# Batched attention-times-value on one core: v loaded in rows of 16 KiB and spread by zero-padded matrices

## Chip, core and metric

The kernel runs on one core of a Trainium2 chip. The metric is the device time in microseconds (us) of one execution; the time of before is the median of three runs.

## The reference

```python
def setup_inputs():
    batch, n_heads, seq, head_dim = 8, 12, 1024, 64
    return {
        "attn_weights": np.random.randn(batch, n_heads, seq, seq).astype(np.float32),
        "v": np.random.randn(batch, n_heads, seq, head_dim).astype(np.float32),
    }

def reference(attn_weights, v):
    return np.einsum('bhqs,bhsd->bhqd', attn_weights, v).astype(np.float32)
```

For each of the 96 heads the kernel multiplies a 1024 x 1024 matrix by a 1024 x 64 matrix, all float32 in memory: 402.7 MB of attention weights and 25.2 MB of v are read, and 25.2 MB of output are written.

## The kernel before

**Units.** The heads are taken in 24 batches (`q`) of four. In a batch each head owns 32 partitions, and each partition holds 32 consecutive query rows of its head. A batch is worked in two units, even and odd (`n` = 0 to 47, `i = n % 2`), of 16 query rows per partition each. `load_attn(n)` (L324) brings a unit's rows as one transfer on Pool's queue that casts from float32 to bfloat16 on its way, 8.4 MB read and 4.2 MB written, into one of two buffers `abf`. Units 46 and 47 are loaded in two halves.

**A unit on TensorE (PE).** `pe_unit` (L186) waits for the unit's load, then transposes it in 16 groups of four matmuls (`transpose_g`, L129, matmuls at L134). VectorE (DVE) and ScalarE (ACT) copy the transposed groups out of PSUM in turns (`copy_g`, L255). PE then transposes the outputs of the unit before back (`transpose_back`, L161), ACT copies these to `osb` (L238), and PE multiplies the transposed weights by v (`multiply`, L176): for each head and each half of the queries eight matmuls accumulate, the two halves going to two halves of the PSUM partitions.

**v.** The matmuls need v as `vbf`, with the position in the sequence, taken modulo eight pieces, on 128 partitions. It is loaded otherwise, in long rows of memory: a partition of `vr` holds 32 consecutive rows of one head, 8 KiB of float32, and a load has two batches side by side (`[P, 2, VB, SB * D]`). `spread_v` (L144) moves it to 128 partitions: for each head, on that head's 32 partitions, four matmuls with 32 x 128 selection matrices (`spread`, of zeros and ones) accumulate in one PSUM bank (L149); the four heads use the four groups of 32 rows of the PE array. It runs once in each even unit, between the unit's transposes and the transposes back. After each head's last matmul `s_sp` goes up by one; DVE copies heads 0 and 2 to `vbf`, ACT heads 1 and 3 (`spread_copy`, L231), and `transpose_back` of that unit waits for all four.

**Pool's queue, in program order.** After the first two attn loads and the selects that build `ident` and `spread`, Pool goes through the units. At an even unit of an odd batch it first waits for that batch's fourth `s_sp`, then issues the next v load (`load_v`, L332, 11 of them); then, for every unit, it waits for DVE's part of the transposes and issues the attn load of two units later. Outputs of eight batches are stored in bursts at batches 8 and 16; the stores of the last batches are issued at the end, on Pool's queue and on SyncE's (SP's).

**The first v.** Its two batches come as float32 on SP's queue, into room of `osb` that is not yet used (`v32`). The first 1 MiB is issued ahead of everything; the memsets of DVE, Pool's selects and ACT's start wait for it. DVE casts it to `vr`. The second 1 MiB is issued by SP after that, and Pool casts it (L382) after it has issued the attn load of unit 2.

Of the kernel before, what the change touches and what calls it, by code (L numbers as in the profile page):

```python
# [10 lines left out]
def kernel(  # L11
# [18 lines left out]
    nc = tc.nc  # L30
    fp32 = mybir.dt.float32
    bf16 = mybir.dt.bfloat16
    PE, DVE, ACT = (getattr(mybir.EngineType, x) for x in ("PE", "DVE", "Activation"))

    B, H, Q, S = attn_weights.shape
    D = v.shape[-1]
    NH = B * H
    P = 128
    VH = 4
    VP = P // VH  # L40
# [2 lines left out]
    HP = P // 2  # L43
    KW = S // (2 * P)
    SB = S // P
    VB = S // VP // SB
    NV = NH // VH
    NU = 2 * NV

# [6 lines left out]
    V_SLOT = 4  # L56
# [5 lines left out]
    def slot(q):  # L62
        return q % NO
# [5 lines left out]
    def out_n(q, fours):  # L69
# [1 line left out]
            "(n four) (p r) d -> (four p) n (r d)", four=VH, p=VP  # L71
        )

    v_2 = v.rearrange("b h q d -> (b h) q d").rearrange(
        "(hq two four) (p r) d -> hq (four p) two (r d)", two=2, four=VH, p=VP
    )

    def on_dve(g):
# [9 lines left out]
    sem = tc.alloc_semaphore  # L88
    sb = lambda name, shape, dt: nc.alloc_sbuf_tensor(name, shape, dt).ap()
    ident = sb("ident", [P, P], fp32)  # L90
    spread = sb("spread", [P, VB, P], bf16)
    abf = [sb(f"abf{i}", [P, G, S], bf16) for i in range(2)]
    at = sb("at", [P, G, KW, P, 2], bf16)
    vr = sb("vr", [P, 2, VB, SB * D], bf16)
    vbf = sb("vbf", [P, SB, VH, D], bf16)
    ot = sb("ot", [P, GH, P], fp32)
    osb = sb("osb", [P, NO, 2 * G, D], fp32)

    v32 = osb[:, ds(V_SLOT, 2)].rearrange("p n r d -> p n (r d)")
    bank = [nc.alloc_psum_tensor(f"bank{i}", [P, 512], fp32).ap() for i in range(8)]  # L100
    pt = [b.rearrange("p (k j) -> p k j", k=KW) for b in bank[:4]]
    po = bank[4:6]
# [2 lines left out]

    s_abf = [sem(f"s_abf{i}") for i in range(2)]
    s_second = {n: sem(f"s_second{n}") for n in range(HALVED, NU)}
    s_v0, s_v = sem("s_v0"), sem("s_v")
    s_osb = sem("s_osb")
    s_held, s_end = sem("s_held"), sem("s_end")  # L110

# [8 lines left out]
    s_const, s_vr = sem("s_const"), sem("s_vr")  # L120

    s_half, s_free = sem("s_half"), sem("s_free")

    nc.sync.dma_start(out=v32[:, 0], in_=v_2[0][:, 0])

    with tc.tile_critical(sync_engine=mybir.EngineType.Pool, no_gpsimd_drain=True):  # L126
        pe = nc.tensor
# [16 lines left out]
        def spread_v(two, banks):  # L144

            for h, ps in enumerate(banks):
                rows = ds(h * VP, VP)
                for b in range(VB):
                    last = pe.matmul(  # L149
                        out=ps,  # L150
                        lhsT=spread[rows, b],
                        rhs=vr[rows, two, b],
                        start=(b == 0),
                        stop=(b == VB - 1),
                    )
                last.then_inc(s_sp)
# [29 lines left out]
        def pe_unit(i, n, both, loaded, it):  # L186

            pe.wait_ge(*loaded)
            for g in range(G):
                if g == GH:  # L190
                    pe.wait_ge(s_half, n)
                transpose_g(abf[i], g, n)
            pe.wait_ge(s_ot, both)
            if i == 0:
                pe.wait_ge(s_vr, it)
                odd = pe.snap((it - 1) % 2)
                with pe.If(odd > 0):
                    spread_v(1, po + px)
                with pe.Else():
                    spread_v(0, po + px)  # L200
                pe.wait_ge(s_vbf, it * 4)
            transpose_back()
            pe.wait_ge(s_last, both)
            for hp in range(2):
                for h in range(2):
                    for half in range(2):
                        outs = po[hp][ds(half * D, D), ds(h * GH * VP, GH * VP)]
                        last = multiply(outs, 2 * hp + h, half)
                last.then_inc(s_m)

        pe.wait_ge(s_const, 3 + VH)
        with nc.Fori(1, NV + 1, 1, engines=(PE,)) as it:
            loaded = pe.snap(it * 16)
            second = pe.snap(it * 2)
# [95 lines left out]
            nc.vector.memset(ot[:, :, ds(h * HP, HP)], 0.0).then_inc(s_ot)  # L310
        for half in range(2):
            last = nc.vector.tensor_copy(
                out=vr[:, 0, ds(half * (VB // 2), VB // 2)].rearrange("p b x -> p (b x)"),
                in_=v32[:, 0, ds(half * (SB * D * VB // 2), SB * D * VB // 2)],
            )
        last.then_inc(s_vr)
        engine(True)
        engine(False)
        nc.scalar.wait_ge(s_held, 16 * (BY_SYNC - HELD_FROM) // 2)
# [2 lines left out]
        pool = nc.gpsimd  # L322

        def load_attn(n):  # L324
            pieces = [(0, G)] if n < HALVED else [(0, GH), (GH, GH)]
            for g0, gn in pieces:
                pool.dma_start(  # L327
                    out=abf[n % 2][:, ds(g0, gn)].rearrange("p g s -> p (g s)"),
                    in_=attn_q[n // 2][:, ds((n % 2 * G + g0) * S, gn * S)],
                ).then_inc(s_abf[n % 2] if g0 == 0 else s_second[n], 16)  # L330

        def load_v(iv):  # L332
            pool.dma_start(  # L333
                out=vr.rearrange("p two b x -> p two (b x)"), in_=v_2[iv]
            ).then_inc(s_v, 16)

        def store(q, fours, eng, done):
            eng.wait_ge(s_out, 2 * (q + fours) + 1)
            at_slot = osb[:, ds(slot(q), fours)].rearrange("p n r d -> p n (r d)")
            eng.dma_start(  # L340
                out=out_n(q, fours), in_=at_slot,
                **({"single_packet": True} if eng is pool and fours == 2 else {}),
            ).then_inc(done, 16)

        def store_2(q):
# [7 lines left out]
            out=ident,  # L353
            in_=ident,
            compare_op=mybir.AluOpType.not_equal,
            fill=1.0,
            base=0,
            pattern=[[-1, P]],
            channel_multiplier=1,
        ).then_inc(s_const)  # L360

        for h in range(VH):
            pool.wait_ge(s_const, h + 3)
            pool.affine_select(  # L364
                out=spread[ds(h * VP, VP)],
                in_=spread[ds(h * VP, VP)],
                compare_op=mybir.AluOpType.not_equal,
                fill=1.0,
                base=0,
                pattern=[[1, VB], [-1, P]],  # L370
                channel_multiplier=VB,
            ).then_inc(s_const)
        for n in range(NU - 2):
            q, i = n // 2, n % 2
            if i == 0 and q % 2 == 1 and q + 1 < NV:
                pool.wait_ge(s_sp, 4 * (q + 1))
                load_v((q + 1) // 2)
            pool.wait_ge(s_t[True], (n + 1) * PER_DVE)
            load_attn(n + 2)
            if n == 0:  # L380
                pool.wait_ge(s_v0, 16)
                pool.tensor_copy(  # L382
                    out=vr[:, 1].rearrange("p b x -> p (b x)"), in_=v32[:, 1]
                ).then_inc(s_vr)
            if i == 0 and q % TOGETHER == 0 and 0 < q <= HELD_FROM:
                for q0, fours in BURSTS[q]:
                    store(q0, fours, pool, s_osb)
# [5 lines left out]

        nc.sync.dma_start(out=v32[:, 1], in_=v_2[0][:, 1]).then_inc(s_v0, 16)
        nc.sync.sem_inc(s_free, NO // 2)
        nc.sync.sem_inc(s_half, HALVED)
        for k in range(1, NV // 2):
# [6 lines left out]
        for n in range(HALVED, NU):  # L406
# [8 lines left out]
            out=out_q[NV - 1], in_=osb[:, slot(NV - 1)].rearrange("p r d -> p (r d)")  # L415
# [35 lines left out]
```

## Time and profile before

| | |
|---|---|
| time, median of 3 runs | 1052.8 us (1052.76 to 1053.04) |
| profiled execution: its own time | 1052.94 us |
| profiled execution: span | 1051.2 us |
| PE busy, mean granted clock | 731.1 us (70%), 0.866 |
| DVE, ACT, Pool busy | 388.2, 410.3, 44.6 us |
| HBM read, written | 427.82 MB, 25.17 MB |
| packets of Pool's queue (q0) | 12832, 99.2% of the 16 DMA engines' span |
| packets of SP's queue (q1) | 848, 1.5% |
| attn load, issue to landing (median) | 30.9 us |
| v load, issue to landing (median) | 12.5 us |

A line of a group gives source line, engine, operation, tiles and shapes, the number of instructions, then busy time in us, the mean of one in ns, and the engine's idle time just before them with what ended it. A line of the timeline gives start and duration in us, and in brackets the idle time before. PEld is PE's loading of weights, which overlaps its matmuls. The queues' lines give packets, MB written and the time of their packets as a share of 16 DMA engines over the span. The sizes of a DMA are those written, after the cast.

### The profile page before, as it was taken

What the parts mean: (1) busy time and instruction counts of PE and PEld (TensorE: products, weight loads), DVE (VectorE), ACT (ScalarE), POOL (GpSimd) and SP (SyncE); (2) the same over time, 40 slices, a digit from 0 to 9 for tenths busy, and PEclk for the clock granted to TensorE, in tenths of its full rate; (3) what the DMA queues carried; (4) which work ended last, traced back from release to release, by engine and by line L of the source; (5) the groups of instructions that cost most, each with busy time, mean ns of one, the idle gap of its engine ahead of it and who ended that gap; (6) DMA issues with size and microseconds to landing.
All of it is one profiled execution on the core that took longest, in us unless ns stands there. A gap on an engine that the chain in (4) does not pass through costs nothing.

```text
span 1051.2 us, 16374 instructions
## 1 busy us (share of the span) xinstructions
PE 731.1 (70%) x6920; PEld 686.2 (65%) x6920; DVE 388.2 (37%) x583; ACT 410.3 (39%) x493; POOL 44.6 (4%) x76
## 2 busy tenths in 40 slices
PE   0877688679579576457957858758716875875985
PEld 0767687578478575457857758658716865875874
DVE  1443344335335333233523434335303433532543
ACT  0444345335335333233533434335304433533543
POOL 2000000000000000000000000001000000000000
PEclk9989889889889898688989889889868988988898
DMA  9999999999999999999999999999999999999998
GB/s 233 227 220 217 218 218 208 216 219 219 219 217 218 216 207 379 219 219 217 217 216 208 219 219 219 207 229 217 359 225 219 219 206 229 218 206 218 218 218 343
DMA packets 13685, 240.19 MB, mean 228 GB/s; under 512 B 1136, under 2 KB 1136, under 8 KB 3952
## 3 DMA queue, kind: packets, MB, share of 16 engines
q0 software_dynamic: 12832, 233.84, 99.2%
q1 hardware_dynamic: 848, 6.29, 1.5%
q8 instruction: 2, 0.03, 0.0%
q14 instruction: 3, 0.02, 0.0%
HBM read 427.82 MB, written 25.17 MB: 431 GB/s over the span
## 4 chain that ended last, share of the span: by engine, by line
DMA 78%; PE 20%; issue 1%; POOL 0%; DVE 0%; ACT 0%; POOLq 0%; SPq 0%
DMA abf<-in_attn_weights_dram 78%; PE bank L134 20%; PE bank L176 0%; PE bank L161 0%; POOL abf L327 0%; DVE osb L238 0%; ACT ot L267 0%; SPq L408 0%; POOLq L435 0%; POOLq L126 0%
## 5 line engine op out<-in xcount | busy, mean ns | idle before, releaser
L134 PE MATMUL bank<-ident,abf 128*128 128x128 f32 x3072 | 446.8, 315 | 277.6 <-DMA abf<-in_attn_weights_dram 273.6
L134 PEld LDWEIGHTS bank<-ident,abf 128*128 128x128 f32 x3072 | 437.3, 214 | 290.4 <-DMA abf<-in_attn_weights_dram 285.8
L255 DVE COPY at<-bank 128x1024 bf16<-128x1024 bf16 x480 | 320.4, 689 | 486.8 <-PE bank L134 484.2
L255 ACT COPY at<-bank 128x1024 bf16<-128x1024 bf16 x288 | 288.8, 1012 | 411.9 <-PE bank L134 411.9
L176 PE MATMUL bank<-at,vbf 128*64 128x256 bf16 x3072 | 215.0, 278 | 0.0
L176 PEld LDWEIGHTS bank<-at,vbf 128*64 128x64 bf16 x3072 | 196.7, 108 | 13.4 <-DVE at L255 4.0
L267 ACT COPY ot<-bank 128x512 f32<-128x512 f32 x48 | 28.1, 586 | 174.0 <-PE bank L176 174.0
L267 DVE COPY ot<-bank 128x512 f32<-128x512 f32 x48 | 33.2, 692 | 151.4 <-PE bank L176 151.4
L161 PE MATMUL bank<-ident,ot 128*128 128x128 f32 x392 | 52.2, 276 | 32.5 <-DVE vbf L231 31.9
L161 PEld LDWEIGHTS bank<-ident,ot 128*128 128x128 f32 x392 | 43.4, 141 | 44.6 <-DVE vbf L231 43.7
L238 ACT COPY osb<-bank 128x512 f32 (+1 forms) x97 | 52.1, 589 | 27.3 <-PE bank L161 26.2
L327 POOL DMA_DIRECT2D abf<-in_attn_weights_dram x50 | 27.1, 542 | 716.9 <-PE bank L134 716.0
L231 DVE CAST vbf<-bank 128x512 bf16<-128x512 f32 x48 | 30.9, 686 | 6.5 <-PE bank L149 6.5
L231 ACT CAST vbf<-bank 128x512 bf16<-128x512 f32 x48 | 25.8, 589 | 11.8 <-PE bank L149 11.8
L149 PE MATMUL bank<-vr,spread 32*128 32x512 bf16 x384 | 26.1, 377 | 0.0
L255 ACT ACT_TABLE_LOAD x12 | 15.4, 1283 | 6.1 <-DMA osb<-in_v_dram 5.9
L333 POOL DMA_DIRECT2D vr<-in_v_dram x11 | 7.7, 703 | 228.7 <-PE bank L149 228.7
L149 PEld LDWEIGHTS bank<-vr,spread 32*128 32x128 bf16 x384 | 11.0, 92 | 6.2
L340 POOL DMA_DIRECT2D out_dram<-osb x5 | 3.9, 785 | 6.9 <-ACT osb L238 6.6
L364 POOL TENSOR_SCALAR_AFFINE_SELECT spread<-spread 32x512 bf16<-32x512 bf16 x4 | 3.6, 900 | 0.6
L306 DVE MEMSET ident<- 128x128 f32 x1 | 0.2, 165 | 5.9 <-DMA osb<-in_v_dram 5.9
L382 POOL CAST vr<-osb 128x2048 bf16<-128x2048 f32 x1 | 1.9, 1883 | 0.0
(9 smaller groups left out, 4.3 us busy)
## 6 DMA issues: line engine op xcount, KB each, us to landing
abf<-in_attn_weights_dram POOLq DMA_DIRECT2D x46, 4096.0 KB, 30.9
vr<-in_v_dram POOLq DMA_DIRECT2D x11, 1024.0 KB, 12.5
out_dram<-osb POOLq DMA_DIRECT2D x1, 8192.0 KB, 44.5
abf<-in_attn_weights_dram POOLq DMA_DIRECT2D x4, 2048.0 KB, 24.0
out_dram<-osb POOLq DMA_DIRECT2D x3, 2048.0 KB, 35.8
out_dram<-osb POOLq DMA_DIRECT2D x1, 6144.0 KB, 44.9
osb<-in_v_dram SPq DMA_DIRECT2D x2, 1024.0 KB, 14.4
out_dram<-osb SPq DMA_DIRECT2D x1, 2048.0 KB, 13.9
```

The lines of the kernel that those rows point to most:

```text
L134: last = pe.matmul(out=pt[g % 4][:, k], lhsT=words[:, k], rhs=ident, is_transpose=True, start=(k == 0), stop=(k == KW - 1),)
L149: last = pe.matmul(out=ps, lhsT=spread[rows, b], rhs=vr[rows, two, b], start=(b == 0), stop=(b == VB - 1),)
L161: last = pe.matmul(out=ps[:, ds(j * P, P)], lhsT=ot[:, j0 + j], rhs=ident, is_transpose=True, start=(j == 0), stop=(j == jn - 1),)
L176: last = pe.matmul(out=outs, lhsT=vbf[:, 2 * kw + par, h], rhs=at[:, ds(half * GH, GH), kw, ds(h * VP, VP), par], start=(n == 0), stop=(n ...
L231: copy(out=vbf[:, :, h], in_=ps.rearrange("p (k d) -> p k d", k=SB)).then_inc(s_vbf)
L238: return copy(out=rows.rearrange("p (half j) d -> p j half d", half=2)[:, ds(j0, jn)], in_=ps[:, ds(0, jn * P)].rearrange("p (j half d) -> ...
L255: ins = copy(out=at[:, g].rearrange("c k j two -> c (k j two)"), in_=bank[g % 4].bitcast(bf16),)
L267: copy(out=ot.rearrange("c j (h p) -> c h j p", h=VH)[:, ds(2 * e, 2)], in_=po[e].rearrange("c (h j p) -> c h j p", h=2, j=GH),).then_inc( ...
L327: pool.dma_start(out=abf[n % 2][:, ds(g0, gn)].rearrange("p g s -> p (g s)"), in_=attn_q[n // 2][:, ds((n % 2 * G + g0) * S, gn * S)],).th ...
L333: pool.dma_start(out=vr.rearrange("p two b x -> p two (b x)"), in_=v_2[iv]).then_inc(s_v, 16)
L340: eng.dma_start(out=out_n(q, fours), in_=at_slot, **({"single_packet": True} if eng is pool and fours == 2 else {}),).then_inc(done, 16)
L364: pool.affine_select(out=spread[ds(h * VP, VP)], in_=spread[ds(h * VP, VP)], compare_op=mybir.AluOpType.not_equal, fill=1.0, base=0, patte ...
```

## The change

A load of v now has eight heads on 128 partitions: 16 partitions a head, each with 64 consecutive rows, 16 KiB of float32 (`v_8`). `vr` loses its dimension of two batches and has eight pieces (`VB` = 8) instead of four. A head's 16 partitions are half of a group of 32, so `spread_v` still takes 32 rows and a selection matrix in which the rows of the other head in that group are zero: `spread` is now `[P, 8, 135]`, one zero-padded band for each of the eight heads, and the matrix for piece `b` is a window of 128 columns in it that starts at `VB - 1 - b`. Each head takes eight matmuls instead of four. In one batch, heads 0 and 1 lie in one group of 32 rows and heads 2 and 3 in another.

The first v comes as one transfer of 2 MiB, ahead of everything, and DVE casts all of it in two instructions of 2048 elements per partition; SP's second transfer and Pool's cast go. One select on Pool over 128 partitions builds `spread` in place of four over 32.

```diff
-    VB = S // VP // SB
+    V8 = 2 * VH
+    VB = S // (P // V8) // SB
+    VR = 32
...
-    v_2 = v.rearrange("b h q d -> (b h) q d").rearrange(
-        "(hq two four) (p r) d -> hq (four p) two (r d)", two=2, four=VH, p=VP
+    v_8 = v.rearrange("b h q d -> (b h) q d").rearrange(
+        "(ho eight) (p r) d -> ho (eight p) (r d)", eight=V8, p=P // V8
     )
...
-    spread = sb("spread", [P, VB, P], bf16)
+    spread = sb("spread", [P, V8, P + VB - 1], bf16)
...
-    vr = sb("vr", [P, 2, VB, SB * D], bf16)
+    vr = sb("vr", [P, VB, SB * D], bf16)
...
-    v32 = osb[:, ds(V_SLOT, 2)].rearrange("p n r d -> p n (r d)")
+    v32 = osb[:, ds(V_SLOT, 2)].rearrange("p n r d -> p (n r d)")
...
-    nc.sync.dma_start(out=v32[:, 0], in_=v_2[0][:, 0])
+    nc.sync.dma_start(out=v32, in_=v_8[0])
...
             for h, ps in enumerate(banks):
-                rows = ds(h * VP, VP)
+                j = two * VH + h
+                rows = ds(j * (P // V8) // VR * VR, VR)
                 for b in range(VB):
                     last = pe.matmul(
                         out=ps,
-                        lhsT=spread[rows, b],
-                        rhs=vr[rows, two, b],
+                        lhsT=spread[rows, j, ds(VB - 1 - b, P)],
+                        rhs=vr[rows, b],
...
-        pe.wait_ge(s_const, 3 + VH)
+        pe.wait_ge(s_const, 4)
...
             last = nc.vector.tensor_copy(
-                out=vr[:, 0, ds(half * (VB // 2), VB // 2)].rearrange("p b x -> p (b x)"),
-                in_=v32[:, 0, ds(half * (SB * D * VB // 2), SB * D * VB // 2)],
+                out=vr[:, ds(half * (VB // 2), VB // 2)].rearrange("p b x -> p (b x)"),
+                in_=v32[:, ds(half * (SB * D * VB // 2), SB * D * VB // 2)],
             )
-        last.then_inc(s_vr)
+        last.then_inc(s_vr, 2)
...
-                out=vr.rearrange("p two b x -> p two (b x)"), in_=v_2[iv]
+                out=vr.rearrange("p b x -> p (b x)"), in_=v_8[iv]
...
-        for h in range(VH):
-            pool.wait_ge(s_const, h + 3)
-            pool.affine_select(
-                out=spread[ds(h * VP, VP)],
-                in_=spread[ds(h * VP, VP)],
+        pool.wait_ge(s_const, 3)
+        pool.affine_select(
+            out=spread,
+            in_=spread,
...
-            if n == 0:
-                pool.wait_ge(s_v0, 16)
-                pool.tensor_copy(
-                    out=vr[:, 1].rearrange("p b x -> p (b x)"), in_=v32[:, 1]
-                ).then_inc(s_vr)
...
-        nc.sync.dma_start(out=v32[:, 1], in_=v_2[0][:, 1]).then_inc(s_v0, 16)
```

More of the change, by code (lines that the diff above doesn't have):

```diff
@@ L107 @@
     s_second = {n: sem(f"s_second{n}") for n in range(HALVED, NU)}
-    s_v0, s_v = sem("s_v0"), sem("s_v")
+    s_v = sem("s_v")
     s_osb = sem("s_osb")
@@ L360 @@
         ).then_inc(s_const)
-        for h in range(VH):
-            pool.wait_ge(s_const, h + 3)
-            pool.affine_select(
-                out=spread[ds(h * VP, VP)],
-                in_=spread[ds(h * VP, VP)],
[L367 to L372, printed above, removed]
+        pool.wait_ge(s_const, 3)
+        pool.affine_select(
+            out=spread,
+            in_=spread,
+            compare_op=mybir.AluOpType.not_equal,
+            fill=1.0,
+            base=VB - 1,
+            pattern=[[-P, V8], [-1, P + VB - 1]],
+            channel_multiplier=VB,
+        ).then_inc(s_const)
         for n in range(NU - 2):
```

## The prediction

> **What bounds the kernel now.** I read the page first (slices and DMA queues), then the chain, then two stretches of the timeline, then the list of who waited for whom.
>
> ```profile
> PE 731.1 (70%) x6920; PEld 686.2 (65%) x6920; DVE 388.2 (37%) x583; ACT 410.3 (39%) x493; POOL 44.6 (4%) x76
> DMA  9999999999999999999999999999999999999998
> q0 software_dynamic: 12832, 233.84, 99.2%
> q1 hardware_dynamic: 848, 6.29, 1.5%
> DMA 78%; PE 20%; issue 1%; POOL 0%; DVE 0%; ACT 0%; POOLq 0%; SPq 0%
> ```
>
> The 16 DMA engines are full in every slice. Bytes confirm it: 427.8 MB read by loads and 25.2 MB stored are 453 MB, 431 GB/s over the span. PE is busy for 70% and waits 273.6 us for attn loads, so PE, DVE and ACT have room, and the time is that of the DMA queue, provided that the queue never runs empty. That proviso is where this change can hurt, so I looked at one v load (unit 26 of 48):
>
> ```profile
> 579.71 10.32 PE L134 MATMUL bank<-ident,abf 128*128 128x128 f32 x64 [4.63 <-DMA abf<-in_attn_weights_dram]
> ...
> 589.96 1.07 PE L149 MATMUL bank<-vr,spread 32*128 32x512 bf16 x16
> ...
> 591.47 0.70 POOL L333 DMA_DIRECT2D vr<-in_v_dram  x1 [20.85 <-PE bank L149]
> 592.17 0.56 POOL L327 DMA_DIRECT2D abf<-in_attn_weights_dram  x1
> 592.38 0.86 PEld L161 LDWEIGHTS bank<-ident,ot 128*128 128x128 f32 x8 [1.84 <-DVE vbf L231]
> ...
> 599.00 1.24 PE L134 MATMUL bank<-ident,abf 128*128 128x128 f32 x8 [1.12 <-DMA abf<-in_attn_weights_dram]
> ```
>
> An attn load lands at 579.7, PE transposes it, spreads v (L149), and only then does Pool issue the next v and, behind it, the next attn load. The load before them lands at 599.0: DMA still had some 7 us of work when v was issued. The packet records say it closer: the first v packet runs 5.8 to 6.2 us after the issue in nine of the eleven loads. In the other two (407 and 756) a store is queued ahead and the figure is 25.8.
>
> ```profile
> L149 PE MATMUL bank<-vr,spread 32*128 32x512 bf16 x384 | 26.1, 377 | 0.0
> L149 PEld LDWEIGHTS bank<-vr,spread 32*128 32x128 bf16 x384 | 11.0, 92 | 6.2
> ...
> vr<-in_v_dram POOLq DMA_DIRECT2D x11, 1024.0 KB, 12.5
> ```
>
> These page lines hold what the change touches: 384 spread matmuls, 16 for each of 24 batches of four heads, together busy for only 26.1 us although one lasts 377 ns, so they overlap; and eleven v loads, 12.5 us from issue to landing, half of it waiting in the queue.
>
> **v's packets.** Eleven loads go from 256 packets (8 KiB read, 4 KiB written) to 128 of twice the size: per engine from 16 to 8. A unit's attn load without v takes 19.3 us (599.00 - 579.71) for 8 packets of 64 KiB per engine, 2.412 us each; with v the step is 24.22 (unit 28 starts at 623.22), so v costs 4.90 us, 0.306 per packet. Bytes are then 37.6 ns per KiB and a packet's own cost is 5 ns. Eight packets fewer save 0.04 us a load, 0.5 us in eleven. The packets' recorded durations (324 ns for 8 KiB, 2432 for 64) would give a fixed part of 23 ns, so 0.18 us a load, 2.0 in all; but recorded packets overlap by 19 ns, so I take the pace: 0.5, with 0 and 2.0 as ends.
>
> **Start.** The first v is issued at 0.74 and L306, L307 and Pool's selects wait for it until 5.9; the second, issued at 5.75 by SP, landed at 29.7 between attn packets. As one transfer of 2 MiB it lands between 7.5 (all eight packets first) and 18 us (half of them alternating with attn packets of 2.4 us). Behind it: DVE's memsets (0.17, spread 0.27 x 1080/512 = 0.6, 1.03) and its cast of four times 1024 elements (0.63 to 1.12 each, 2.5 to 4.5), at most 6.3 us; Pool's selects 0.28 and one of 1080 elements at 0.9 per 512, 1.9 instead of 3.6. All done by 24.5 at the latest; unit 0's load lands at 27.1, unchanged since the same bytes precede it. Pool's 1.88 us cast at 38.19 and SP's second issue go. Cost 0; the cover is 2.6 us at worst.
>
> **The spread on PE.** This is the change's real cost. Now there are 16 matmuls on four row groups, one head each. The records show them interleaved: four streams, each with a matmul every 0.216 us, the last ones starting at 0.66 to 0.79 us, the four signals 1.05 to 1.22 us after the start. After, a batch has 32 matmuls on two row groups: h0 and h1 share one, h2 and h3 the other, 16 matmuls in each. Side by side that is 16 x 0.216 + 0.2 = 3.7 us; one after the other 32 x 0.216 + 0.2 = 7.1. Which? The nearest row is L176, eight matmuls to one half of the columns, then eight to the other: in the records the second half's first matmul starts 0.47 us after the first's, when the fifth of eight has begun and three still wait. So PE looks past about three waiting matmuls of a busy group, not past sixteen. Then h2 starts when 13 of the 16 have started, at 2.6 us, and the last signal comes at 2.6 + 3.46 + 0.2 = 6.2 us. I take 6.2, 5.0 more than now; ends 2.5 and 5.9 more.
>
> The Trainium skill, TensorE: Matmul & The Clock Gate, Part 3, speaks against the change: small-K matmuls gain by lying in distinct row groups (four tiles 3.07 times), and here half the groups are given up. It also has matmuls start strictly in program order; by that the spread would be the 7.1 us. The interleaved starts here disagree with that.
>
> PE's path: the copies of h0 to h2 go under the spread, and only ACT's copy of h3 (0.59) follows, so the transposes back start 6.95 instead of 2.42 us after the spread's start: 4.5 us more in every even unit. PE now ends such a unit about 1.1 us before the next landing (599.00 row); it will start the odd unit 3 us late. The odd unit, 13.3 to 14.8 us long in steps of 19.3 to 24.2, takes that up: 0 on the path. Its attn issue moves from 570.1 to about 571.1 to 573, with some 7 us of queue left.
>
> **Pool's issue.** In 11 even units the v load waits for the fourth spread signal, with attn's load queued behind it on Pool: both 5.0 us later. Cover was 5.9; 0.9 remains. Two things add to it. PE's idle time before unit 26 (4.6 us) shrinks to about 3.5, since the odd unit before it starts without a pause; its transposes then run partly at full clock (8.03 us in warm units against 10.3 here), worth 0 to 1.1 us, say 0.7. And two engines run 1.0 us behind the other fourteen (a load's 16 signals spread over 1.2 us), which the fourteen may lose at no cost. So an issue may take 0.9 + 0.7 + 1.0 = 2.6 us to its first packet at no cost. What it takes is not shown with an empty queue: SP's first v took 1.0 us (0.74 to 1.76), Pool's first attn load at most 3.4 (1.34 to 4.77, partly behind v). I take 2.2, the middle: covered, 0.
>
> By the Trainium skill, DMA: Bandwidth & Descriptors, Specifications, the first byte of a GpSimd-issued DMA comes after about 1 us; by that the cover holds with ease. No row here shows that 1 us.
>
> **Tail.** Unit 46's work now ends at 1023.97 and the last half load lands at 1029.9. With 4.5 us more, the last unit's halves are transposed back to back and the last store's issue moves from 1041.93 to about 1044.6. Its first packet, 1.0 us on, is at 1045.6; the stores ahead fill most engines until 1045.5 (packets end at 1047.9, less eight of 0.306). Cost 0, up to 0.6.
>
> **Sum.** The profiled execution took 1052.94 (span 1051.2 and 1.7 around it), 0.14 over the median. 1052.94 - 0.5 = 1052.4; for the median 1052.3. A measurement of this kernel can tell about 0.2%, 2.1 us.
>
> **Rivals.**
> *The DMA queue runs dry at v loads (slower).* If the first packet comes over 2.6 us after Pool's issue, each of nine v loads leaves all engines empty for the difference. At 3.1 us (Pool's first load, less a packet already under way) that is 0.5 x 9 = 4.5 us; without the clock's 0.7, 1.2 x 9 = 11; with matmuls in order (0.9 less cover) 2.1 x 9 = 19. For it: the 3.4 us row, the sole row of Pool's latency. Against: that was Pool's first DMA, with v's packets ahead of it. Time 1055 to 1071, most likely 1059. It decides where issue to first packet passes the cover.
> *Packets cost what their durations say (faster).* 2.0 us saved and the lagging engines catching up: 1050 to 1051. Against: the 24.22 step leaves v only 0.08 us above its bytes.
> *The rows are cut again into 8 KiB packets.* Then nothing is saved: 1052.8. Attn packets of 64 KiB read speak against it.
>
> **Chances.** No change beyond 0.2%: 0.60, likeliest value 1052.3 (own range 1050.9 to 1054.0), the cut rows within it. The dry queue: 0.33. Packets by duration: 0.07. The range reaches from 1050.7 to 1062, which leaves out the dry queue's worst forms.
>
> **What would show it.** L149: 768 matmuls, busy near 24 x 6.2 = 150 us (88 if side by side, 170 in order). v's issue to landing falls from 12.5 to about 7 us. L134's step over a v load stays 24.2; over 24.5, or DMA slices under 9, means the queue ran dry and the forecast is wrong. Odd units start without waiting for their load. The first store on SP after 1044 and the end within 0.6 us of 1051.

## The result and the profile after

The changed kernel takes 1070.9 us (median of six runs, 1064.63 to 1073.56) against 1052.84 (1052.76 to 1053.04): 1.0159 times the time of before, 95% interval 1.0138 to 1.018. The prediction said 1052.3 with a range up to 1062: wrong. The profiled execution took 1071.71 us, its span is 1069.2, 18.0 more than before.

Lines of the page of the changed kernel, in the order of those shown of before:

```profile
PE 895.3 (84%) x7304; PEld 741.6 (69%) x7304; DVE 391.4 (37%) x583; ACT 413.5 (39%) x493; POOL 39.5 (4%) x72
PEclk9898798788888888688888888888878888888888
DMA  9999999999999999999999999999999999999997
q0 software_dynamic: 11424, 233.84, 98.1%
DMA 59%; PE 39%; issue 1%; POOL 1%; ACT 0%; DVE 0%; POOLq 0%
L152 PE MATMUL bank<-vr,spread 32*128 32x512 bf16 x768 | 180.3, 423 | 0.0
L336 POOL DMA_DIRECT2D vr<-in_v_dram x11 | 5.9, 533 | 231.0 <-PE bank L152 231.0
vr<-in_v_dram POOLq DMA_DIRECT2D x11, 1024.0 KB, 9.8
```

The packets went as planned: 1408 fewer on Pool's queue (12832 to 11424). The spread, now L152, is busy for 180.3 us instead of 26.1, or 7.5 per even unit. In the chain DMA gave way to PE, 39% instead of 20%. The DMA slices still say 9 everywhere but at the end: a gap of one or two microseconds doesn't show in a slice of 27.

It shows in a stretch of the timeline. This is an even unit of an odd batch (unit 10), PE and Pool of the changed kernel, then the same unit in the kernel before, and below it the busy time of the engines of the changed kernel in three stretches, of which the middle one follows the issue of v; its columns are span, engines, granted clock, DMA share and GB/s. The last line is a stretch of the kernel before.

```profile
235.38 7.95 PE L136 MATMUL bank<-ident,abf 128*128 128x128 f32 x64 [0.22 <-DMA abf<-in_attn_weights_dram]
243.27 8.81 PE L152 MATMUL bank<-vr,spread 32*128 32x512 bf16 x32
252.75 1.97 PE L164 MATMUL bank<-ident,ot 128*128 128x128 f32 x8 [0.68 <-ACT vbf L234]
...
252.38 0.53 POOL L336 DMA_DIRECT2D vr<-in_v_dram  x1 [21.67 <-PE bank L152]
252.90 0.54 POOL L330 DMA_DIRECT2D abf<-in_attn_weights_dram  x1
```

```profile
231.34 10.41 PE L134 MATMUL bank<-ident,abf 128*128 128x128 f32 x64 [4.61 <-DMA abf<-in_attn_weights_dram]
...
243.19 0.70 POOL L333 DMA_DIRECT2D vr<-in_v_dram  x1 [20.91 <-PE bank L149]
```

```profile
243.00:251.00 8.00, 8.00 (x33) 3.18 (x33) 2.30 (x4) 1.49 (x2) 0.00 (x0) 0.73 0.91 197
252.00:254.50 2.50, 1.82 (x9) 1.57 (x8) 0.00 (x0) 1.09 (x2) 1.06 (x2) 0.50 0.50 46
255.00:263.00 8.00, 8.00 (x88) 7.38 (x87) 2.28 (x4) 2.66 (x4) 0.00 (x0) 0.88 1.13 238
```

```profile
247.00:249.50 2.50, 2.50 (x40) 2.27 (x36) 0.69 (x1) 0.00 (x0) 0.00 (x0) 1.00 0.45 95
```

Pool waits for the spread until 252.38, 17.0 us after the landing; before, it issued at 11.9 in this unit. The DMA share between 252.0 and 254.5 is 0.50, but that alone doesn't prove a gap: the view counts a packet, with all its time, in the stretch in which it starts, and the kernel before shows 0.45 in a stretch (247.0 to 249.5) in which its packet records leave no engine idle. The records of the changed kernel decide: from 252.0 to 253.5 some 9 to 13 of the 16 engines have no packet, and the gap comes to 1.5 us on the average of all 16. The queue does run empty. So the rival "the DMA queue runs dry at v loads" came true. In the landing signals of the trace the step over this v load is 26.8 us instead of 24.2.

Where the 18.0 us lie: SP issues the first of its stores as soon as the last half attn load has landed, at 1045.66 instead of 1030.05, so 15.6 us are lost up to there; 2.4 come after it (23.5 us to the end instead of 21.1), where the last store is issued 18.8 us after that landing instead of 11.9. By the landing signals, 9.7 of the 15.6 us lie in the steps over the eleven v loads (276.1 us in sum instead of 266.4), 3.4 in other steps, 2.3 of these in the two next to the bursts of stores, 1.9 in the last two half loads, and 0.5 at the start.

A dry spell costs more than its gap. The step over this v load is 2.7 us longer with 1.5 us of idle engines, and packets that start after the gap run longer: v's first ones 0.8 to 2.0 us here instead of 0.62, attn packets up to 3.78 us instead of 2.43. Up to the last attn landing the engines were idle 5.4 us longer, and their packets took 10 us longer, than in the kernel with alternating heads below, which moves the same packets. Why packets run longer after a gap, no run shows.

### The profile page after: what moved, and what is told of

It is laid out like the page before. It is cut to its first block, busy times and chain, and to the rows that moved or that the text cites. A ratio compares the mean times of both kernels' runs of the same rounds, so it can differ in the third digit from the quotient of the medians.

```text
span 1069.2 us, 17134 instructions
## 1 busy us (share of the span) xinstructions
PE 895.3 (84%) x7304; PEld 741.6 (69%) x7304; DVE 391.4 (37%) x583; ACT 413.5 (39%) x493; POOL 39.5 (4%) x72
## 3 DMA queue, kind: packets, MB, share of 16 engines
q0 software_dynamic: 11424, 233.84, 98.1%
## 4 chain that ended last, share of the span: by engine, by line
DMA 59%; PE 39%; issue 1%; POOL 1%; ACT 0%; DVE 0%; POOLq 0%
DMA abf<-in_attn_weights_dram 59%; PE bank L136 23%; PE bank L152 11%; PE bank L179 4%; PE bank L164 1%; POOL vr L336 1%; ACT vbf L234 0%; DVE osb L241 0%; ACT ot L270 0%; POOLq L431 0%; POOLq L128 0%
## 5 line engine op out<-in xcount | busy, mean ns | idle before, releaser
L136 PE MATMUL bank<-ident,abf 128*128 128x128 f32 x3072 | 409.2, 298 | 151.5 <-DMA abf<-in_attn_weights_dram 151.5
L136 PEld LDWEIGHTS bank<-ident,abf 128*128 128x128 f32 x3072 | 400.1, 211 | 162.4 <-DMA abf<-in_attn_weights_dram 157.6
L179 PE MATMUL bank<-at,vbf 128*64 128x256 bf16 x3072 | 243.1, 300 | 0.0
L179 PEld LDWEIGHTS bank<-at,vbf 128*64 128x64 bf16 x3072 | 215.3, 117 | 26.9 <-issue 7.9
L152 PE MATMUL bank<-vr,spread 32*128 32x512 bf16 x768 | 180.3, 423 | 0.0
L152 PEld LDWEIGHTS bank<-vr,spread 32*128 32x128 bf16 x768 | 67.9, 100 | 94.3 <-issue 27.9
L164 PE MATMUL bank<-ident,ot 128*128 128x128 f32 x392 | 73.2, 349 | 16.9 <-ACT vbf L234 16.2
L164 PEld LDWEIGHTS bank<-ident,ot 128*128 128x128 f32 x392 | 60.5, 182 | 38.3 <-ACT vbf L234 37.4
L258 ACT ACT_TABLE_LOAD x12 | 15.4, 1283 | 18.7 <-DMA osb<-in_v_dram 18.5
L309 DVE MEMSET ident<- 128x128 f32 x1 | 0.2, 165 | 18.5 <-DMA osb<-in_v_dram 18.5
L315 DVE CAST vr<-osb 128x2048 bf16<-128x2048 f32 x2 | 3.3, 1672 | 0.0
L366 POOL TENSOR_SCALAR_AFFINE_SELECT spread<-spread 128x1080 bf16<-128x1080 bf16 x1 | 2.5, 2507 | 0.1
```

The costliest lines, as they stand in the source:

```text
L136: last = pe.matmul(out=pt[g % 4][:, k], lhsT=words[:, k], rhs=ident, is_transpose=True, start=(k == 0), stop=(k == KW - 1),)
L152: last = pe.matmul(out=ps, lhsT=spread[rows, j, ds(VB - 1 - b, P)], rhs=vr[rows, b], start=(b == 0), stop=(b == VB - 1),)
L164: last = pe.matmul(out=ps[:, ds(j * P, P)], lhsT=ot[:, j0 + j], rhs=ident, is_transpose=True, start=(j == 0), stop=(j == jn - 1),)
L179: last = pe.matmul(out=outs, lhsT=vbf[:, 2 * kw + par, h], rhs=at[:, ds(half * GH, GH), kw, ds(h * VP, VP), par], start=(n == 0), stop=(n ...
L258: ins = copy(out=at[:, g].rearrange("c k j two -> c (k j two)"), in_=bank[g % 4].bitcast(bf16),)
L315: last = nc.vector.tensor_copy(out=vr[:, ds(half * (VB // 2), VB // 2)].rearrange("p b x -> p (b x)"), in_=v32[:, ds(half * (SB * D * VB / ...
```

## The experiments

"Late issue" is the theory that the long spread holds back Pool's two issues and the queue runs dry. The lead of an issue is the time by which it precedes the end of the work already queued; in the packet records it is the time from the issue to the first v packet, as long as this directly follows the last attn packet of an engine. The rivals of late issue: the 16 KiB transfers themselves cost time, or PE, 84% busy, has become the bound.

**PE's part alone, on the transfers of before.**

```diff
-                rows = ds(h * VP, VP)
-                for b in range(VB):
+                rows = ds((two * 2 + h // 2) * VP, VP)
+                for b in range(2 * VB):
...
-                        lhsT=spread[rows, b],
-                        rhs=vr[rows, two, b],
+                        lhsT=spread[rows, b % VB],
+                        rhs=vr[rows, two, b % VB],
```

> The kernel before, its v loads and first v untouched, but its spread made as long as in the changed kernel: each head's four matmuls are issued twice and two heads share a group of 32 rows (32 matmuls on two groups; the values are not the reference's). Late issue (the spread holds back Pool's v load and the attn load behind it, the DMA queue runs dry, and PE drops to half clock inside the spread): as slow as the changed kernel, 1063 to 1074 us, v steps of 25 to 27 us. Transfers (16 KiB rows cost DMA time): 1052.8, since the rows are still 8 KiB.

Measured: 1067.97 us (1062.22 to 1076.89), ratio 1.0159, interval 1.0109 to 1.021: the whole loss with rows of 8 KiB. From its page:

```profile
PE 900.4 (85%) x7304; PEld 742.3 (70%) x7304; DVE 388.8 (37%) x583; ACT 413.9 (39%) x493; POOL 44.6 (4%) x76
L149 PE MATMUL bank<-vr,spread 32*128 32x512 bf16 x768 | 185.4, 432 | 0.0
vr<-in_v_dram POOLq DMA_DIRECT2D x11, 1024.0 KB, 8.8
```

**The transfers alone, with a spread as short as before.**

```diff
-                rows = ds(j * (P // V8) // VR * VR, VR)
-                for b in range(VB):
+                rows = ds(h * VR, VR)
+                for b in range(VB // 2):
```

> The changed kernel with all of its transfers, but a spread as short as before: four matmuls a head instead of eight, each head on its own group of 32 rows (it leaves out half of v's pieces). Late issue: 1052.3 us, 0.5 under before, which is the packets' saving alone; v step 24.18. Transfers: 1065 to 1073, as the changed kernel. Saving by the packets' recorded durations: 1050.8.

Measured: 1052.68 us against 1052.97, ratio 0.9997, interval 0.9988 to 1.0006. The transfers cost nothing; a saving of 0.3 us is within the noise. The transfers are out as a cause.

**PE's work kept, only its order changed.** Heads 0 and 2, then 1 and 3, alternate; the copies' waits follow (`s_sp` at 2 and 4), and DVE now copies heads 0 and 1, ACT heads 2 and 3.

```diff
-            for h, ps in enumerate(banks):
...
-                for b in range(VB):
+            for pair in ((0, 2), (1, 3)):
+                for b in range(VB):
+                    for h in pair:
```

> The changed kernel with the same 32 matmuls in another order: heads 0 and 2 alternate, then heads 1 and 3, so that both groups of 32 rows are fed from the start. Late issue: the spread takes 3.7 us at full clock, up to 5 if the clock drops; v is issued 12 to 13 us after the landing, well ahead of 17.9: 1052.0 to 1053.0 us, 0.5 under before if the tail is covered. Transfers: 1065 to 1073. PE too full: between, about 1058, as PE loses 3.8 us of work in each of 24 units.

Measured: 1053.12 us against 1052.97, ratio 1.0002, interval 0.9993 to 1.0011. The same 32 matmuls take 3.63 us, Pool issues v 13.2 to 13.6 us after the landing, a little later than expected, and the loss is gone:

```profile
589.47 3.63 PE L153 MATMUL bank<-vr,spread 32*128 32x512 bf16 x32
...
593.43 0.53 POOL L338 DMA_DIRECT2D vr<-in_v_dram  x1 [23.50 <-PE bank L153]
```

**PE's order and work kept, only Pool's order changed.**

```diff
-            if i == 0 and q % 2 == 1 and q + 1 < NV:
-                pool.wait_ge(s_sp, 4 * (q + 1))
-                load_v((q + 1) // 2)
             pool.wait_ge(s_t[True], (n + 1) * PER_DVE)
             load_attn(n + 2)
+            if i == 0 and q % 2 == 1 and q + 1 < NV:
+                pool.wait_ge(s_sp, 4 * (q + 1))
+                load_v((q + 1) // 2)
```

> The changed kernel with two requests on Pool in another order: in an even unit of an odd batch the attn load of two units later is issued before Pool waits for the spread and issues v; PE's work and all transfers are the same. Late issue on Pool: attn is issued 8.3 us after the landing instead of 15 to 18, DMA has work all the time, v steps return to 24.2 us; what stays is the end, where the last store comes late (2 to 3 us), and odd units whose own attn load is issued late (up to 3 us together): 1054 to 1060. PE too full, or transfers: 1065 to 1073.

Measured: 1053.41 us against 1052.91, ratio 1.0005, interval 0.9996 to 1.0015. Page and Pool's timeline of this kernel:

```profile
PE 908.4 (86%) x7304; PEld 746.3 (71%) x7304; DVE 392.2 (37%) x583; ACT 413.2 (39%) x493; POOL 39.5 (4%) x72
```

```profile
589.67 0.53 POOL L330 DMA_DIRECT2D abf<-in_attn_weights_dram  x1 [18.39 <-PE bank L136]
597.86 0.53 POOL L336 DMA_DIRECT2D vr<-in_v_dram  x1 [7.65 <-PE bank L152]
```

PE is busier than in the changed kernel, 908 us, and the time is that of before: PE is not the bound. Attn is issued as soon as the transposes are done, v 8.2 us later, behind it. Less stayed than expected: the end cost nothing either, although the last store is issued 15.6 us after the last landing (11.9 before), as other stores still fill the queue.

**The clock.** The same 32 matmuls on all 128 rows:

```diff
-                rows = ds(j * (P // V8) // VR * VR, VR)
+                rows = ds(0, P)
```

> The changed kernel with the spread's matmuls on all 128 rows (the zero-padded matrices are zero for the other heads' rows), 32 matmuls one after the other: 7.1 us at full clock, longer than the 6.2 us that the changed kernel's spread takes at full clock. Late issue with the clock as part of the cause (matmuls on one group of 32 rows let PE's clock drop): the clock holds, the spread is 7.1 us every time instead of 6.2 to 9.0, Pool issues v 15.4 us after the landing, first packets at 16.6 to 17.7 where 17.9 is needed: 1053 to 1058 us. Late issue without the clock's part (clock drops for another reason): 1070 or more. Transfers, or PE being too full: 1065 to 1073.

Measured: 1066.77 us, ratio 1.0129, interval 1.0105 to 1.0152. The clock did hold, the spread takes 6.9 or 7.1 us every time; the time did not come down to 1058 but lies in the range written for the rivals, transfers or a full PE, which the runs above rule out. PE now idled 2 to 3 us ahead of the even units with a v load, the transposes of eight of these eleven ran partly at half clock (9.2 to 9.4 us instead of 7.95), and Pool's issue came 15.2 to 16.7 us after the landing, as late as in the changed kernel (14.6 to 17.2). So the clock's drop inside the spread is real, and the loss comes without it too when the issue is late; what the drop costs by itself this run doesn't show.

**A length between.**

```diff
-                for b in range(VB):
+                for b in range(VB + 4):
...
-                            lhsT=spread[rows, j, ds(VB - 1 - b, P)],
+                            lhsT=spread[rows, j, ds(VB - 1 - b % VB, P)],
```

> A length between: the alternating order with twelve matmuls a head instead of eight, four of them repeated (the values are not the reference's), 24 on each of two groups, 5.4 us at full clock, against 3.7 (no loss) and 6.2 to 9.0 (18 us lost). Late issue: v is issued about 15 us after the landing, at the edge between the changed kernel's loads that lost nothing (14.6 to 15.1) and those that did (15.3 and later): 1053 to 1058. A loss in proportion to PE's work: 1061 to 1063, halfway.

Measured: 1062.23 us (1061.33 to 1064.04), ratio 1.0093, interval 1.0078 to 1.0109. From its PE and Pool timelines:

```profile
596.12 5.35 PE L153 MATMUL bank<-vr,spread 32*128 32x512 bf16 x48
601.80 0.53 POOL L338 DMA_DIRECT2D vr<-in_v_dram  x1 [25.00 <-PE bank L153]
```

The spread is 5.35 us each time and v is issued 14.7 to 16.2 us after the landing. The forecast's count gave 5.4 us as nearly free; 9 us are lost, and the time falls into the range of the rival, a loss in proportion to PE's work. This run by itself speaks for the rival; the kernel with Pool's order changed (PE busy for 908 us, no loss) and the one with selects of 2700 elements below (PE busy for 730 us, 15 lost) speak against the rival. So the next question was the lead that an issue needs.

**Pool's issue alone.** The kernel before, with an idle select on Pool between the wait and the v load:

```diff
                 pool.wait_ge(s_sp, 4 * (q + 1))
+                pool.affine_select(out=idle, in_=idle, ..., pattern=[[-1, 1290]], ...).then_inc(s_idle)
+                pool.wait_ge(s_idle, (q + 1) // 2 + 1)
                 load_v((q + 1) // 2)
```

> The kernel before, with nothing of PE, v or the attn loads changed: ahead of each v load Pool runs a select over a tile that nobody reads, 1290 elements, about 3.0 us (0.2 more to signal), so that v and the attn load behind it are issued 3.2 us later and lead the end of the queued work by some 2.8 us instead of 6.0. If an issue needs 2.2 us of lead, as the forecast had it: 1052.9. If it needs about 3, as the loads of the changed kernel suggest (no loss at a lead of 2.9 and more, 1 us lost at about 1.3): 1053 to 1056.

> The same with 2150 elements, about 5.0 us on Pool, the length that the forecast gave the spread: the lead is 0.8 us in nine of eleven loads. Late issue: 1 to 2 us lost at each, 1062 to 1071 us, with PE as before (731 us busy). PE too full: 1052.9.

Measured: 1052.78 and 1052.75 us, ratios 1.0 and 1.0001. Neither tested what it was for: the selects take 1.26 and 1.97 us, since I had scaled a duration of another select. By the packet records the leads were 4.1 to 4.7 us with 1290 elements, 4.3 to 4.7 in seven and 3.2 in two of the nine loads with 2150. Such leads are free, and so is a select on Pool by itself. Then two selects in a row, with the select of the sizes named:

> As the two kernels with a select on Pool, whose selects ran faster than expected (1.3 and 2.0 us, 0.3 to signal: leads of 4.4 and 3.7 us, no loss). Now two selects of 1720 elements, 3.8 us in all, which leave a lead of 2.2 us in nine of eleven v loads. An issue that needs 2.2, as forecast: 1052.9. One that needs about 3: 0.5 to 0.9 us lost at each, 1056 to 1061.

> Two selects of 2700 elements, 5.4 us in all, lead 0.6 us, PE, v and attn loads as before. Late issue: 1 to 2 us lost at each of nine loads, 1062 to 1071 us, with PE still busy for some 731 us. PE too full: 1052.9.

Measured: 1054.18 us, ratio 1.0015, interval 1.0004 to 1.0026, and 1068.01 us (1066.6 to 1070.82), ratio 1.0148, interval 1.013 to 1.0166. The second one's page, Pool's timeline and two stretches around one v load:

```profile
PE 729.8 (68%) x6920; PEld 684.8 (64%) x6920; DVE 387.6 (36%) x583; ACT 410.0 (38%) x493; POOL 100.5 (9%) x99
L383 POOL TENSOR_SCALAR_AFFINE_SELECT idle<-idle 128x2700 bf16<-128x2700 bf16 x22 | 53.5, 2430 | 234.6 <-PE bank L151 233.0
```

```profile
599.60 5.01 POOL L383 TENSOR_SCALAR_AFFINE_SELECT idle<-idle 128x2700 bf16<-128x2700 bf16 x2 [20.83 <-PE bank L151]
604.90 0.72 POOL L335 DMA_DIRECT2D vr<-in_v_dram  x1 [0.30 <-POOL idle L383]
605.62 0.55 POOL L329 DMA_DIRECT2D abf<-in_attn_weights_dram  x1
```

```profile
602.00:604.00 2.00, 2.00 (x35) 1.95 (x34) 0.00 (x0) 0.50 (x2) 1.85 (x2) 1.00 1.14 246
604.00:606.00 2.00, 2.00 (x33) 1.82 (x28) 0.69 (x1) 0.00 (x0) 1.70 (x3) 1.00 0.09 16
```

PE has the same work as before (730 us), v has its old rows, and 15 us are lost by Pool's issue alone. By the packet records the first v packet comes 1.4 us after the issue at 604.90, and the engines are idle for 1.1 us on average around it. Up to the last attn landing they are idle 5.4 us longer than in the kernel before, and their packets, the same ones, take 9.6 us longer. This is the cause, shown by itself.

The kernel with 1720 elements did not test a lead of 2.2 us either, since its selects take 1.62 us each: the first v packet ran 2.5 to 3.3 us after the issue, directly behind the last attn packet. That lost next to nothing: the steps over the eleven v loads sum to 266.65 us instead of 266.40, and the rest of the 1.1 us that the profiled execution lost lies mostly in the two steps with bursts of stores. In the traces of all kernels, leads of 2.5 us and more lost at most 0.2 us a load, leads of 2.1 to 2.4 between 0.2 and 1.8, and shorter ones between nothing and 3.1. So a lead of about 2.5 us is safe; 3 is not needed.

**Both repairs.**

> Both repairs, alternating order and attn ahead of v on Pool. Late issue: nothing is left to win beside the packets, 1052.4 to 1053.1, the same as before within 0.1%.

Measured: 1052.91 us against 1052.91, ratio 0.9999, interval 0.999 to 1.0008. No version here is measurably faster than the kernel before.

## Why the prediction was wrong, point by point

- **What bounds the kernel, and the danger named:** right. The DMA queue sets the time as long as it never runs empty; the change hurt by exactly this proviso.
- **v's packets, 0.5 us saved:** right in kind, about half in size. In the two kernels with the new transfers and a short spread the steps over the eleven v loads sum to 266.1 us instead of 266.4. The recorded durations' 2.0 us did not come.
- **Start, 0:** right for the total within the noise, not for its terms. v landed at 18.5 us (forecast 7.5 to 18), and unit 0's load, forecast as unchanged, lands 0.6 us later in the kernels with this start.
- **The spread, 6.2 us:** the order was right to the matmul: in the records of the changed kernel the second group starts with the thirteenth matmul of the first. The size was not: 7.5 us on average, 6.4 to 9.0. In all 24 spreads the granted clock falls to half 3.3 to 5.9 us after the start, and the start-to-start time goes from 0.216 to 0.427 us. The clock, which the forecast only entered as a gain, was a loss here too. That runs of this kernel differ by 9 us among themselves fits with where the clock's windows happen to fall; no run tested that.
- **PE's path, 0:** right; PE at 908 us costs nothing with Pool's order repaired.
- **Pool's issue, 0: the step that failed.** The forecast let an issue take 2.6 us at no cost and so called it covered. The issue came about when forecast, 16.0 us after the landing on average over the nine loads (14.6 to 17.2), where the terms give 16.3 (17.9 less 0.9 and 0.7). That was luck: the transposes ran at full clock in all these units, 7.95 us instead of some 10.3, where only 0.7 was entered, and the longer spread took this back.

  The 2.2 us for what an issue takes was near the 2.5 that the runs show to be safe. What was wrong is the third term of the 2.6, the 1.0 us for the lagging engines. It was no gift: the 16 landing signals of one load, 1.1 to 1.4 us apart before, spread over up to 3.1, which fits with engines that get their first packets one after the other, 1.2 to 2.3 us after the issue; and the slowest engine times the next landing. Some loads were spared by the lag (in the kernel with 24 matmuls on each group, four with first packets 1.2 to 1.5 us after the issue lost at most 0.1 us in their own step), but not each by 1.0. Without this term the forecast's own figures leave 1.6 us where 2.2 are taken, 0.6 short at each of nine loads, or 5.4 us. Six of the nine did lose.

  The price was too low as well, in the rival too: it counts the empty time only, and packets that run longer after the gap cost more than the gap.
- **The Trainium skill's two rules.** In the Trainium skill, TensorE: Matmul & The Clock Gate, Part 3, small-K matmuls gain by lying in distinct row groups; the traces agree, with 1.07 us for 16 matmuls on four groups and 3.63 for 32 on two, alternating. Its strict program order is contradicted by the changed kernel, where the second group's first matmul, the 17th in the program, starts 8 ns after the 13th, at 2.61 us, while the 14th to 16th still wait. The alternating kernel doesn't bear on the order, since its pairs start in program order. The Trainium skill, DMA: Bandwidth & Descriptors, Specifications, gives about 1 us to the first byte of a GpSimd-issued DMA; the first of sixteen engines agrees (1.23 us), but the last starts at 2.3, and a lead of 1 us does not keep the queue full.
- **Tail, 0 to 0.6:** 2.4 in the changed kernel, where the last spread took 8.9 us instead of 6.2 and the transposes back and the multiply behind it ran partly at half clock; in the kernel with Pool's order repaired it was 0.
- **Chances:** 0.33 went to the case that came. Its price was given as 4.5, 11 and 19 us. That 18 lies near the worst form, which the range left out, is luck: 19 was for matmuls in order, which did not come, and for empty time alone.

## What to carry to other kernels

Where a queue is full, count the lead of every issue over the end of the queued work, and treat that lead as the resource a change spends: some 6 us more on an engine with 30% to spare cost 18 us because one in-order queue waited for it with a load behind. Put the request that doesn't depend on the long step ahead of the one that does, and feed row groups in turn rather than head after head. Don't count the slack of lagging engines as cover, and price a dry queue at more than its empty time. And read a dry queue from packet records or landing steps, not from the DMA share of a short stretch.

## What the runs showed of the hardware that was not expected

- PE's clock fell to half within each of the 24 spreads of 32-row matmuls on one group after the other, 3.3 to 5.9 us after the start (start-to-start 427 ns after 216). It held through spreads of 7.1 us when the matmuls used all 128 rows, and through 5.35 us with two groups at once. The mean granted clock over the run was 0.852, 0.917 and 0.902.
- A load issued by Pool to idle DMA engines started after 1.2 us on the first engine and about 2.3 on the last, and packets after the gap ran longer (v's first ones 0.6 to 2.0 us instead of 0.62); with a lead of 2.5 us or more, a v load lost at most 0.2 us.
- A select on Pool is not linear through zero, nor the same by shape: 0.90 us for 32 x 512, 2.51 for 128 x 1080 with two dimensions of pattern, but 1.26 for 128 x 1290 and 1.97 for 128 x 2150 with one.
